# Tokens in the order of their groups: two tiles normed among the experts, two at the end

## The chip, the cores and the metric

The kernel runs on one core of a Trainium2 chip. The metric is the device time of one launch in microseconds (us). The core has a matrix engine, TensorE (PE, with its weight loads PEld), and VectorE (DVE), ScalarE (ACT) and GpSimd (POOL); SyncE (SP) issues most transfers, and 16 DMA engines move them. Each engine and each queue works its instructions off in order; engines wait for one another by semaphores. SBUF is the memory beside the engines (128 partitions), PSUM takes TensorE's results (banks of 512 fp32 columns on 128 partitions).

## The reference

One layer of an encoder over 512 tokens of 1024 values in fp32, normed after each part: two kinds of attention and their projections, a norm, and then a mixture of experts and the second norm. What matters here is the second half:

```python
def _hierarchical_moe(x, ...):          # x: 512 x 1024, after the first norm
    g_sel = top_k(softmax(x @ w_group + b_group), 1)          # 1 group of 4, its probability g_val
    top_w = softmax(top_k(e_logits of that group, 2))         # 2 experts of its 8
    for g in range(4):
        hid = silu(x @ w_gate[g]) * (x @ w_up[g])             # 8 experts, 256 wide
        y = y + (hid * combine[:, g]) @ w_down[g]
x = _layer_norm(ALPHA * x + y, ln2_g, ln2_b)
```

A token thus goes to two experts of one group. The 32 experts' weights (3 MB each, 96 MB in all) are all read.

## The kernel before

The attention part, the first norm and the routing take the first 410 us or so and stay as they are, apart from a few rows of the routing. The normed tokens (over ALPHA's scale, with what the end needs) lie in `hD` in DRAM, by token. `finish_routing()` works out for each expert the list of its tokens (at most 64 slots; more in any expert sets `flag`, and a dense way is then taken at the end). `toki` and `rowi` hold, for each pair of experts `p` (128 slots), the row in `hD` that a slot reads and the row in `y2D` that it writes. `y2D` has two rows for each token, one for each of its experts, zeroed at the start.

The experts follow in order, `for e in range(NE)`. Their weights come as six loads of 512 KB each: four for gate and up, two for down, in the order of the list `seq`, issued by SP and with `AHEAD` loads allowed ahead (`weights`, `raw_load`). For an expert TensorE does `gate_up(e)` (16 matmuls into a bank `sc`; ACT and DVE bring it out and add its halves into `gus`), `down(e - 1)` (8 matmuls into `tr`; ACT and DVE bring it out, scaled by the routing weight, into `oe`), at every odd expert `prep_x` (the gathered rows `xg` of the next pair are transposed into a bank `pj`, and ACT and DVE copy it to `xp`), and `act(e)` (four transposes of `gus` into `stp`, then `sg`, SiLU on ACT and a product on DVE). GpSimd gathers `xg` for a later pair (`fetch`) and after each pair scatters `oe` to `y2D`. `pin` and `in_order` fix the order of instructions; what isn't pinned the scheduler may place. The last two pairs (experts 28 to 31) don't go through DRAM: their results `late` stay in SBUF, and matmuls by one-hot matrices `stl` add them to their tokens.

The end works by tiles of 128 tokens. SP loads the residual rows `hb` of the four tiles after expert 20's part of the program (`HB_AT`) and, behind all weights, the eight tiles of rows `yy` of `y2D` (`last_rows`). Eight PSUM banks `fin` hold the four tiles (two banks a tile). An order written out by hand, `FIN`, adds into them by matmuls: `hb` by the identity, `late` of each of the four last experts by `stl`, and the sum of a tile's two `yy` tiles, added on GpSimd for tiles 0 to 2 and left to the matmuls for tile 3. Behind each tile comes its norm: statistics, root and two gain steps on DVE (`stat`, `gain`, `root`), the root's Ln and Exp on ACT; the last step of tiles 0 to 2 is on ACT and GpSimd, of tile 3 on DVE. SP writes the tiles out.

Of the kernel before, what the change touches and what calls it, by code (L numbers as in the profile page):

```python
# [94 lines left out]
).split()  # L95
# [10 lines left out]
def trunk(ctx, tc, xT, x, wm, wv, wbr, wout, wr, br, bg, rbx, lnp, lncol, wexp, out):  # L106
# [36 lines left out]
    hD = dram.tile([S, D], F32, name="hD")  # L143

# [522 lines left out]
    val = small([P, TT, 2], "val", at=end0)  # L667
    tokv = small([P, TT, 2], "tokv", at=end0)
# [59 lines left out]
    iota([P, TT, 2], [[2 * P, TT], [1, 2]], -2 * S, 2, "val", val)  # L728
# [145 lines left out]
    def route(tt):  # L874
# [7 lines left out]
        m = small([P, 4], f"m{tt}")  # L882
# [20 lines left out]
        mm(rk, tri, MS[:, tt, :], False, True)  # L903
        pm = small([P, 2, NE], f"pm{tt}")
# [12 lines left out]
    def finish_routing():  # L917
# [10 lines left out]

        pmf = B8[:, :2].rearrange("p q t k n -> p (q t k n)").rearrange("p (k t e) -> p k t e", k=2, t=TT)
# [33 lines left out]
        cn = pp.tile([P, NE], F32, tag="av", name="cn", bufs=AVB)  # L963
        for u in range(TT):
            mm(cn, ones, MS[:, u, :], u == 0, u == TT - 1)
        V.tensor_reduce(out=mx, in_=cn, axis=AX.X, op=OP.max)
        V.tensor_scalar(out=flag, in0=mx, scalar1=CAP + 0.5, scalar2=None, op0=OP.is_gt)
# [72 lines left out]
    for e in range(NE + 1):  # L1040
        seq += [(e, c) for c in range(4) if e < NE] + [(e - 1, 4 + f) for f in range(2) if e > 0]
# [79 lines left out]
    def gate_up(e):  # L1121
# [11 lines left out]
        nc.scalar.activation(gus[e], ps[CAP:], AF.Copy)  # L1133
        nc.vector.tensor_add(gus[e], gus[e], ps[:CAP])  # L1134
# [3 lines left out]
    def act(e):  # L1138
# [13 lines left out]
    def down(e):  # L1152
# [21 lines left out]
        if odd and p < NPAIR - NLATE:  # L1174
            nc.gpsimd.indirect_dma_start(  # L1175
                out=y2D[:, :], out_offset=bass.IndirectOffsetOnAxis(ap=rowi[:, p : p + 1], axis=0),
                in_=oe[p], in_offset=None, bounds_check=2 * S - 1, oob_is_err=False,
            )

    res, fs, fr, fu, parts = {}, {}, {}, {}, {}  # L1180
    stl = []
    gb2 = []
    late = []

    def last_rows():

        tok3 = bp.tile([P, 2 * NLATE], F32, tag="tok3", name="tok3", bufs=1)
        nc.vector.tensor_scalar(out=tok3, in0=tok2, scalar1=-256.0, scalar2=None, op0=OP.add)
        for n in range(NLATE):
            st = lop.tile([P, 2, 2, 256], F32R, tag="lo", name=f"stl{n}")  # L1190
            for k in range(2):
                i = k * NLATE + n
                for q, tok in enumerate((tok2, tok3)):
                    nc.vector.tensor_scalar(
                        out=st[:, k, q], in0=iota256, scalar1=tok[:, i : i + 1], scalar2=None, op0=OP.is_equal
                    )
                stl.append(st[:, k].rearrange("p q s -> p (q s)"))
        for tt in range(TT):
            y2.append([slot([P, D], F32, f"yy{tt}{k}") for k in range(2)])
            for k in range(2):  # L1200
                nc.sync.dma_start(y2[tt][k], y2v[tt, k])
# [14 lines left out]
    y2, hb = [], []  # L1216
    fin, added = {}, {}

    def fin_open(n):
        tt, cs = n // 2, slice(n % 2 * S, n % 2 * S + S)  # L1220
        fin[n] = pb.tile([P, S], F32, tag=FIN_TAG[n], name=f"fin{n}", bufs=NBUF[FIN_TAG[n]])
        mm(fin[n], ident, hb[tt][:, cs], True, False)
        added[n] = 0
# [225 lines left out]
```

## Time and profile before

| | |
|---|---|
| median of the runs | 688.9 us (688.48 to 690.85, 3 runs) |
| the profiled execution | 689.27 us, its span 687.6 us |
| busy in the span | PE 647.6 us (94%), DVE 393.4 (57%), ACT 312.1 (45%), POOL 102.5 (15%) |
| mean granted clock of TensorE | 0.985 |
| DMA | 160.17 MB, mean 233 GB/s; SP's queue 152.26 MB, POOL's 7.31 MB |

The span runs from the first to the last instruction; the run's time has some more around it. Busy shares are means over stages that differ: the DMA moves little in the first half and 400 GB/s and more among the experts.

### The profile page before, as it was taken

What the parts mean: (1) busy time and instruction counts of PE and PEld (TensorE: products, weight loads), DVE (VectorE), ACT (ScalarE), POOL (GpSimd) and SP (SyncE); (2) the same over time, 40 slices, a digit from 0 to 9 for tenths busy, and PEclk for the clock granted to TensorE, in tenths of its full rate; (3) what the DMA queues carried; (4) which work ended last, traced back from release to release, by engine and by line L of the source; (5) the groups of instructions that cost most, each with busy time, mean ns of one, the idle gap of its engine ahead of it and who ended that gap; (6) DMA issues with size and microseconds to landing.
All of it is one profiled execution on the core that took longest, in us unless ns stands there. A gap on an engine that the chain in (4) does not pass through costs nothing.

```text
span 687.6 us, 8900 instructions
## 1 busy us (share of the span) xinstructions
PE 647.6 (94%) x3128; PEld 422.8 (61%) x3128; DVE 393.4 (57%) x820; ACT 312.1 (45%) x618; POOL 102.5 (15%) x149
## 2 busy tenths in 40 slices
PE   8999999999999999989999988999999988899992
PEld 4888788887878888878888775343333422223351
DVE  5675868678867887563854994233233322224256
ACT  5676877866755665644523222222222322222232
POOL 2012112102010110050000331211111111000043
PEclk9999999999999999999999999899999999999997
DMA  8600069103130322126793579999999999999923
GB/s 329 253 1 0 1 227 353 63 0 93 47 107 17 123 76 93 37 97 260 264 362 125 177 290 399 407 410 409 409 411 407 408 408 408 402 411 409 407 96 123
DMA packets 48320, 160.17 MB, mean 233 GB/s; under 512 B 7438, under 2 KB 7582, under 8 KB 48272
## 3 DMA queue, kind: packets, MB, share of 16 engines
q1 hardware_dynamic: 44208, 152.26, 58.0%
q0 software_dynamic: 4064, 7.31, 2.8%
q8 instruction: 26, 0.43, 0.3%
q14 instruction: 22, 0.18, 0.1%
HBM read 151.20 MB, written 15.73 MB: 243 GB/s over the span
## 4 chain that ended last, share of the span: by engine, by line
PE 60%; DVE 15%; DMA 14%; ACT 6%; issue 3%; POOL 0%; SPq 0%; DVEq 0%; POOLq 0%; ACTq 0%
PE pj L132 18%; PE sc L132 13%; DMA we<-in_wexp_dram 11%; PE pb L132 6%; PE tr L132 6%; PE po L132 4%; PE pv L132 2%; PE fin L132 2%; PE av L132 2%; DVE t L484 2%; DVE wl L117 2%; DMA hb<-hD 2%; PE tr L538 2%; DMA raw<-in_wm_dram 2%; ACT wh L114 1%
## 5 line engine op out<-in xcount | busy, mean ns | idle before, releaser
L132 PE MATMUL sc<-we,xp 128*64 128x512 f32 x448 | 107.8, 604 | 4.0 <-DMA we<-in_wexp_dram 3.4
L132 PE MATMUL pj<-xh,wh 128*128 128x512 f32 x256 | 103.5, 404 | 1.2 <-ACT wh L114 1.1
L132 PE MATMUL pj<-xh,wl 128*128 128x512 f32 x256 | 101.0, 394 | 0.2 <-DVE wl L117 0.2
L132 PE MATMUL pj<-xl,wh 128*128 128x512 f32 x256 | 100.9, 394 | 0.2 <-DVE xl L117 0.2
L117 DVE TENSOR_TENSOR wl<-raw,wh 128x1024 fp32r<-128x1024 f32 (+1 forms) x57 | 69.9, 1231 | 22.8 <-ACT wh L114 22.6
L1134 DVE TENSOR_TENSOR gus<-gus,sc 64x512 f32<-64x512 f32 x32 | 21.7, 679 | 97.7 <-ACT gus L1133 97.7
L132 PE MATMUL tr<-we,sg 128*64 128x512 f32 x256 | 64.5, 614 | 6.9 <-DMA we<-in_wexp_dram 5.1
L1133 ACT ACTIVATE gus<-sc 64x512 f32<-64x512 f32 x32 | 19.0, 593 | 109.2 <-PE sc L132 109.2
L114 ACT ACTIVATE wh<-raw 128x1024 fp32r<-128x1024 f32 (+1 forms) x57 | 58.7, 1037 | 18.8 <-DMA raw<-in_wbr_dram 4.8
L132 PEld LDWEIGHTS sc<-we,xp 128*64 128x64 f32 x448 | 27.5, 136 | 59.5 <-issue 29.0
L132 PEld LDWEIGHTS pj<-xh,wl 128*128 128x128 f32 x256 | 48.4, 189 | 11.5 <-DVE wl L117 1.1
L132 PEld LDWEIGHTS pj<-xh,wh 128*128 128x128 f32 x256 | 48.5, 189 | 10.8 <-ACT wh L114 1.6
L132 PEld LDWEIGHTS pj<-xl,wh 128*128 128x128 f32 x256 | 48.5, 190 | 9.1 <-DVE xl L117 0.9
L132 PEld LDWEIGHTS tr<-we,sg 128*64 128x64 f32 x256 | 16.9, 139 | 47.1 <-issue 32.3
L132 PE MATMUL pb<-y,wh 128*128 128x512 f32 x128 | 40.0, 394 | 0.3 <-DVE k L347 0.3
L117 DVE TENSOR_TENSOR wl<-tr,wh 128x512 fp32r<-128x512 f32 (+1 forms) x64 | 30.9, 485 | 11.9 <-ACT wh L114 11.6
L491 POOL TENSOR_SCALAR_AFFINE_SELECT w<-w 128x128 f32<-128x128 f32 x32 | 16.1, 514 | 125.5 <-ACT w L488 117.8
L114 ACT ACTIVATE wh<-tr 128x512 fp32r<-128x512 f32 (+1 forms) x64 | 27.2, 427 | 12.4 <-PE tr L538 12.2
L1175 POOL DMA_INDIRECT y2D<-oe,rowi x14 | 14.1, 1010 | 118.9 <-DVE oe L1173 91.4
L132 PE MATMUL sc<-k,q 128*128 128x512 f32 (+3 forms) x128 | 28.5, 323 | 0.2
L538 PE MATMUL tr<-ident,w 128*128 128x128 f32 x160 | 27.8, 272 | 0.0
L132 PEld LDWEIGHTS pb<-y,wh 128*128 128x128 f32 x128 | 23.3, 188 | 5.0 <-PE tr L538 0.5
(226 smaller groups left out, 1188.1 us busy)
## 6 DMA issues: line engine op xcount, KB each, us to landing
we<-in_wexp_dram SPq DMA_DIRECT2D x192, 512.0 KB, 11.2
raw<-in_wm_dram SPq DMA_DIRECT2D x32, 512.0 KB, 6.2
raw<-in_wv_dram SPq DMA_DIRECT2D x8, 512.0 KB, 8.7
y2D<-zero SPq DMA_DIRECT2D x16, 256.0 KB, 4.2
raw<-in_wbr_dram SPq DMA_DIRECT2D x8, 512.0 KB, 5.0
raw<-in_wout_dram SPq DMA_DIRECT2D x8, 512.0 KB, 4.9
yy<-y2D SPq DMA_DIRECT2D x8, 512.0 KB, 10.1
strip<-in_rbx_dram SPq DMA_DIRECT2D x8, 256.0 KB, 4.7
```

The lines of the kernel that those rows point to most:

```text
L114: act = nc.scalar.activation(hi, src, AF.Copy)
L117: pin((eng or nc.vector).tensor_sub(lo, src, hi.bitcast(F32)), fix == "both")
L132: pin(nc.tensor.matmul(ps, a, b, start=start, stop=stop))
L484: nc.vector.tensor_tensor_scan(out=t[:, ::-1], data0=t[:, ::-1], data1=mk[:, ::-1], initial=0.0, op0=OP.add, op1=OP.mult)
L491: nc.gpsimd.affine_select(out=blk, in_=blk, pattern=[[-1, P]], compare_op=OP.is_gt, fill=0.0, base=0, channel_multiplier=1)
L538: nc.tensor.transpose(tr[:, i * P : (i + 1) * P], w[:, off + j * P : off + (j + 1) * P], ident)
L1133: nc.scalar.activation(gus[e], ps[CAP:], AF.Copy)
L1134: nc.vector.tensor_add(gus[e], gus[e], ps[:CAP])
L1175: nc.gpsimd.indirect_dma_start(out=y2D[:, :], out_offset=bass.IndirectOffsetOnAxis(ap=rowi[:, p : p + 1], axis=0), in_=oe[p], in_offset=No ...
```

## The change

Positions of tokens are now sorted by group: the routing counts the tokens of each group, and a token's position is the number of tokens in earlier groups plus its rank among its own. `y2D`'s rows, the one-hot matrices for the late experts and the tiles of the end go by positions. So tiles 0 and 1 hold tokens of the first groups only, whose experts are done long before the end. `tokD` in DRAM keeps which token stands at a position (four small scatters at experts 4 to 10, read back at 13 as `tokp`). All row loads move from SP to GpSimd's queue: residual rows are gathered by `tokp`, tiles 0 and 1 with their `y2D` rows at experts 23 and 26, tiles 2 and 3 at 28 and 29. Tiles 0 and 1 are summed and normed on DVE at experts 26 and 28 and scattered to the output by GpSimd; only tiles 2 and 3 stay for the end, with four banks, into which the late experts and, for each tile, one sum of rows are added. The last three experts' down weights are loaded behind expert 31's gate and up weights. Outputs of `gate_up`, `act` are now pinned. The dense way is also taken where the first two groups have under 128 tokens or the first three under 256.

```diff
+ROWS_AT = {23: 0, 26: 1}
+NORM_AT = {26: 0, 28: 1}
+GAIN_AT = 21
+OUT_AT = {28: 0, 30: 1}
+TOKD_AT = {4: 0, 6: 1, 8: 2, 10: 3}
+TOKP_AT = 13
...
+        cn = pp.tile([P, NE], F32, tag="av", name="cn", bufs=AVB)
+        for u in range(TT):
+            mm(cn, ones, MS[:, u, :], u == 0, u == TT - 1)
+        V.tensor_reduce(out=cg, in_=cn.rearrange("p (g e) -> p g e", g=4), axis=AX.X, op=OP.add)
...
+        V.tensor_add(p2[:, 0], p2[:, 0], p2[:, 1])
+        V.tensor_tensor(out=val, in0=last(p2[:, 0], 2), in1=k01, op=OP.add)
...
-    for e in range(NE + 1):
-        seq += [(e, c) for c in range(4) if e < NE] + [(e - 1, 4 + f) for f in range(2) if e > 0]
+    for e in range(NE):
+        seq += [(e, c) for c in range(4)] + [(e - 1, 4 + f) for f in range(2) if 0 < e < NE - 2]
+    seq += [(e, 4 + f) for e in range(NE - 3, NE) for f in range(2)]
...
-        nc.scalar.activation(gus[e], ps[CAP:], AF.Copy)
-        nc.vector.tensor_add(gus[e], gus[e], ps[:CAP])
+        pin(nc.scalar.activation(gus[e], ps[CAP:], AF.Copy))
+        pin(nc.vector.tensor_add(gus[e], gus[e], ps[:CAP]))
...
-                nc.sync.dma_start(y2[tt][k], y2v[tt, k])
...
+    def tile_rows(tt, pool):
+        for y, k, where in ((ya, 0, pool), (yb, 1, slots2)):
+            y[tt] = slot([P, D], F32, f"y{k}{tt}", where)
+            tc.keep_in_program_order(nc.gpsimd.dma_start(y[tt], y2v[tt, k]))
...
+    def tile_sum(tt, eng):
+        pin(eng.tensor_add(ya[tt], ya[tt], hb[tt]))
+        pin(eng.tensor_add(ya[tt], ya[tt], yb[tt]))
...
+        act(e)
+        if e in ROWS_AT:
+            tile_res(ROWS_AT[e])
+            tile_rows(ROWS_AT[e], slots2)
+        if e in NORM_AT:
+            t = NORM_AT[e]
+            tile_sum(t, nc.vector)
+            tile_norm(t, (ya[t][:, :S], ya[t][:, S:]), "vector")
+        if e in OUT_AT:
+            tile_out(OUT_AT[e])
...
+    tile_sum(2, nc.vector)
+    tile_sum(3, nc.gpsimd)
+    down(NE - 2)
...
+    for n in range(2):
+        mm(fin[n], ident, ya[2][:, n * S : n * S + S], False, False)
+    down(NE - 1)
```

On DVE, the first place is experts 26 and 27. Before, the sum `gus` of expert 26 is the first row and that of expert 27 the fourth; the copy `xp` for experts 28 and 29 comes behind both:

```order
L1134 TENSOR_TENSOR gus<-gus,sc 64x512
L1173 TENSOR_SCALAR oe<-tr,wslot 64x512
L1147 TENSOR_TENSOR sg<-sg,stp 128x128
L1134 TENSOR_TENSOR gus<-gus,sc 64x512
L1173 TENSOR_SCALAR oe<-tr,wswap 64x512
L1088 COPY xp_5457<-pj 128x512
L1147 TENSOR_TENSOR sg<-sg,stp 128x128
```

After, `gus`, `oe` and `sg` of expert 26 are as before (not shown), and then comes this, where `y_5434` is tile 0 (the rows of its first expert, to which its residual `hb_5430` and the rows of its second expert `y_5436` are added):

```order
L1122 COPY xp_5592<-pj 128x512
L1258 TENSOR_TENSOR y_5434<-y_5434,hb_5430 128x1024
L1259 TENSOR_TENSOR y_5434<-y_5434,y_5436 128x1024
L1268 BN_STATS bsf<-y_5434 128x6 x2
L1269 BN_AGGR mv<-bsf 128x2
L1270 TENSOR_SCALAR mv<-mv 128x1
L1274 SCALAR_TENSOR_TENSOR y_5434<-y_5434,mv,gb_5274 128x512 x2
L1277 SCALAR_TENSOR_TENSOR mv<-mv 128x1
L1278 TENSOR_SCALAR mv<-mv 128x1
L1279 TENSOR_TENSOR mv<-mv 128x1
L1285 SCALAR_TENSOR_TENSOR y_5434<-y_5434,mv,gb_5303 128x512 x2
L1168 TENSOR_TENSOR gus<-gus,sc 64x512
```

The copy `xp` has moved from behind expert 27's `gus` to ahead of tile 0's eleven rows, and `gus` of expert 27, the last row here, stands behind them all.

On GpSimd, the end of the expert loop before: the last gather, three scatters of pairs, and the sums of `yy` of three tiles:

```order
L1092 DMA xg_3019<-hD,toki 128x1024
L1175 DMA y2D<-oe,rowi 1024x1024 x3
L1242 TENSOR_TENSOR yy_5578<-yy_5578,yy_5579 128x1024
L1242 TENSOR_TENSOR yy_5582<-yy_5582,yy_5583 128x1024
L1242 TENSOR_TENSOR yy_5586<-yy_5586,yy_5587 128x1024
```

After, from the last gather (`hb_5430`, `y_5434`, `y_5436` belong to tile 0, `hb_5547`, `y_5551`, `y_5553` to tile 1, the next two to tiles 2 and 3):

```order
L1126 DMA xg_3027<-hD,toki 128x1024
L1251 DMA hb_5430<-hD,tokp 128x1024
L1247 DMA y_5434<-y2D 128x1024
L1247 DMA y_5436<-y2D 128x1024
L1251 DMA hb_5547<-hD,tokp 128x1024
L1208 DMA y2D<-oe,rowi 1024x1024 x2
L1290 DMA out_dram<-y_5434,tokp 512x1024
L1247 DMA y_5551<-y2D 128x1024
L1247 DMA y_5553<-y2D 128x1024
L1251 DMA hb_5672<-hD,tokp 128x1024
L1251 DMA hb_5676<-hD,tokp 128x1024
L1208 DMA y2D<-oe,rowi 1024x1024
```

Row loads that stood in SP's queue now stand between gathers and scatters. Tile 0's output (`out_dram`) is ahead of tile 1's rows, and the scatter of a pair is behind both.

On PE, the end after, from the transposes of the last expert's `gus` (`we_5439` is the down weight of expert 30, `we_5447` that of 31, `y_5723` tile 2):

```order
L1175 MATMUL stp<-ident,gus 128x64 x4
L125 MATMUL tr<-we_5439,sg 64x512 x2
L125 MATMUL tr<-we_5443,sg 64x512 x2
L125 MATMUL fin_5743<-late_5774,stl 128x512
L125 MATMUL fin_5745<-late_5774,stl 128x512
L125 MATMUL fin_5747<-late_5774,stl 128x512
L125 MATMUL fin_5749<-late_5774,stl 128x512
L125 MATMUL fin_5743<-y_5723,ident 128x512
L125 MATMUL fin_5745<-y_5723,ident 128x512
L125 MATMUL tr<-we_5447,sg 64x512 x2
```

Tile 2's two identity matmuls stand ahead of the down matmuls of expert 31; before, in that place, stood nothing between the down matmuls of experts 30 and 31.

## Rows read from the trace of the kernel before

**Rows 1.** Windows of the experts' stretch and of one us after the last load.
```profile
420.00:640.00 220.00, 206.18 (x998) 73.90 (x996) 67.81 (x134) 57.90 (x116) 28.36 (x28) 0.98 1.03 408
...
662.00:663.00 1.00, 1.00 (x5) 0.63 (x4) 0.00 (x0) 0.00 (x0) 0.08 (x1) 1.00 0.00 0
```

**Rows 2.** PE's timeline, experts 4 to 6: start, us, engine, line, operation, tiles.
```profile
447.94 1.09 PE L1107 MATMUL pj<-ident,xg 128*128 128x128 f32 x8
...
455.04 3.65 PE L132 MATMUL sc<-we,xp 128*64 128x512 f32 x16
458.52 1.89 PE L132 MATMUL tr<-we,sg 128*64 128x512 f32 x8
460.34 1.09 PE L1107 MATMUL pj<-ident,xg 128*128 128x128 f32 x8
```

**Rows 3.** SP's timeline from 400 us: its DMA issues.
```profile
410.03 197.01 SPq L1052 DMA_DIRECT2D we<-in_wexp_dram  x142
607.97 4.08 SPq L1327 DMA_DIRECT2D hb<-hD  x4
614.19 27.90 SPq L1052 DMA_DIRECT2D we<-in_wexp_dram  x22
643.04 9.29 SPq L1201 DMA_DIRECT2D yy<-y2D  x8
```

**Rows 4.** DMA issues: size of one, median us from issue to landing.
```profile
we<-in_wexp_dram SPq DMA_DIRECT2D x192, 512.0 KB, 11.2
...
yy<-y2D SPq DMA_DIRECT2D x8, 512.0 KB, 10.1
...
out_dram<-res SPq DMA_DIRECT2D x3, 512.0 KB, 2.6
...
xg<-hD,toki POOLq DMA_INDIRECT x14, 7.3
```

**Rows 5.** DVE's timeline of the end.
```profile
659.55 0.76 DVE L120 SCALAR_TENSOR_TENSOR late<-tr,wslot,late 64x512 fp32r<-64x512 f32 x1 [0.75 <-ACT late L119]
664.45 0.70 DVE L1264 BATCH_NORM_STATS2 bsf<-fin 128x6 f32<-128x512 f32 x1 [4.14 <-PE fin L132]
...
667.05 0.21 DVE L787 SCALAR_TENSOR_TENSOR mv<-mv 128x1 f32<-128x1 f32 x1
...
668.10 0.69 DVE L1264 BATCH_NORM_STATS2 bsf<-fin 128x6 f32<-128x512 f32 x1
...
678.93 1.12 DVE L787 SCALAR_TENSOR_TENSOR mv<-mv 128x1 f32<-128x1 f32 x1
...
681.01 1.41 DVE L1290 SCALAR_TENSOR_TENSOR res<-res,mv,gb 128x512 f32<-128x512 f32 x2
```

**Rows 6.** POOL's timeline: the first gather, the last one, adds at the end.
```profile
430.66 1.10 POOL L1092 DMA_INDIRECT xg<-hD,toki  x1 [14.51 <-DVE rowi L949]
...
580.78 1.01 POOL L1092 DMA_INDIRECT xg<-hD,toki  x1 [6.35 <-PE pj L1107]
...
677.55 2.48 POOL L1299 TENSOR_TENSOR res<-res,gb 128x512 f32<-128x512 f32 x2 [1.76 <-ACT res L1298]
```

**Rows 7.** PE's timeline, experts 26 and 27, and expert 31's down.
```profile
610.61 2.22 PE L132 MATMUL tr<-we,sg 128*64 128x512 f32 x8 [0.29 <-DMA we<-in_wexp_dram]
...
613.79 0.46 PE L1141 MATMUL stp<-ident,gus 64*128 64x64 f32 x4
...
655.35 1.94 PE L132 MATMUL tr<-we,sg 128*64 128x512 f32 x8 [1.49 <-DVE sg L1147]
```

**Rows 8.** Groups of instructions by form, DVE: adds of 128x1024 from SBUF.
```profile
L117 DVE TENSOR_TENSOR wl<-raw,wh 128x1024 fp32r<-128x1024 f32 x55 | 68.7, 1251 | 22.3 <-ACT wh L114 22.1
```

**Rows 9.** ACT's timeline of the end: a table load.
```profile
654.38 1.28 ACT L1145 ACT_TABLE_LOAD   x1
```

**Rows 10.** Windows with the granted clock, after two idle times of PE.
```profile
431.00:437.00 6.00, 5.19 (x18) 1.75 (x20) 1.49 (x6) 1.74 (x7) 2.74 (x3) 0.50 1.03 408
...
654.00:656.00 2.00, 0.65 (x4) 0.34 (x6) 1.03 (x2) 1.97 (x4) 1.31 (x1) 1.00 0.99 393
```

More of the change, by code (lines that the diff above doesn't have):

```diff
@@ L962, in finish_routing @@
         nc.scalar.activation(wswap[HD:, :], wslot[:HD, :], AF.Copy)
[L963 to L967, printed above, removed]
+        V.tensor_scalar(out=posf, in0=p2[:, 0], scalar1=0.5, scalar2=1.0 * S, op0=OP.mult, op1=OP.add)
+        V.tensor_scalar(out=mx, in0=mx, scalar1=CAP + 0.5, scalar2=None, op0=OP.is_gt)
+        for k, n in ((2, 2 * P), (3, 4 * P)):
+            V.tensor_scalar(out=few[:, k - 2 : k - 1], in0=sp[:, k : k + 1], scalar1=n - 0.5, scalar2=None, op0=OP.is_lt)
+            V.tensor_tensor(out=mx, in0=mx, in1=few[:, k - 2 : k - 1], op=OP.max)
+        V.tensor_scalar(out=flag, in0=mx, scalar1=0.5, scalar2=None, op0=OP.is_gt)
         for tt in range(TT):
@@ L1174, in down @@
         if odd and p < NPAIR - NLATE:
-            nc.gpsimd.indirect_dma_start(
+            tc.keep_in_program_order(nc.gpsimd.indirect_dma_start(
                 out=y2D[:, :], out_offset=bass.IndirectOffsetOnAxis(ap=rowi[:, p : p + 1], axis=0),
                 in_=oe[p], in_offset=None, bounds_check=2 * S - 1, oob_is_err=False,
[L1178 to L1200, printed above, removed]
-                nc.sync.dma_start(y2[tt][k], y2v[tt, k])
+            ))
+    late, gb2, stl = [], [], []
     def gain_rows():
@@ L1214, in gain_rows @@
                 nc.scalar.activation(gb2[k][:, j * S : j * S + S], ps, AF.Copy)
[L1216 to L1223, printed above, removed]
-    def fin_add(n, upto):
-        tt, cs = n // 2, slice(n % 2 * S, n % 2 * S + S)
-        for k in range(added[n], upto):
-            end = k == 2 * NLATE - 1 and FIN.index(f"add{n}.{k + 1}") > FIN.index(f"rows{tt}")
-            mm(fin[n], stl[k][:, tt * P : (tt + 1) * P], late[k][:, cs], False, end)
-        added[n] = upto
@@ new lines, in late_slots @@
+    def late_slots():
+        st = lop.tile([P, 2 * NLATE, 2 * P], F32R, tag="lo", name="stl")
+        for n in range(NLATE):
+            for k in range(2):
+                i = k * NLATE + n
+                one = st[:, 2 * n + k]
+                V.tensor_scalar(out=one, in0=iota256, scalar1=tok2[:, i : i + 1], scalar2=None, op0=OP.is_equal)
+                V.scalar_tensor_tensor(
+                    out=one, in0=iota256, scalar=tok3[:, i : i + 1], in1=one.bitcast(F32), op0=OP.is_equal, op1=OP.add
+                )
+                stl.append(st[:, 2 * n + k])
@@ new lines, in tile_out, with fin_add @@
+    def tile_out(tt):
+        tc.keep_in_program_order(nc.gpsimd.indirect_dma_start(
+            out=out[:, :], out_offset=bass.IndirectOffsetOnAxis(ap=tokp[:, tt : tt + 1], axis=0),
+            in_=ya[tt], in_offset=None, bounds_check=S - 1, oob_is_err=False,
+        ))
+    fin = []
+    def fin_add(n, k):
+        if len(fin) <= n:
+            fin.append(pb.tile([P, S], F32, tag=FIN_TAG[n], name=f"fin{n}", bufs=NBUF[FIN_TAG[n]]))
+        mm(fin[n], stl[k][:, n // 2 * P : (n // 2 + 1) * P], late[k][:, n % 2 * S : n % 2 * S + S], k == 0, k == 2 * NLATE - 1)
```

203 lines of the change are left out of this document (109 added, 94 removed), and 6 rows, old and new, of the table FIN.

## The prediction

> **What bounds the kernel now.** I read the windows first, because the experts are a stage of their own. From 420 to 640 us the DMA engines are busy all the time at 408 GB/s [rows 1], and TensorE (PE) idles only in short waits for a weight tile. A 512 KB load therefore takes 524,288 / 408,000 = 1.285 us of the core's DMA time, and a pair of experts (12 loads) 15.4 us, while PE, where the weights are there, does a pair in 12.4 us (from one transpose of gathered rows to the next, 447.94 to 460.34) [rows 2]. So PE has a slack of some 3 us a pair, or a little more once PE's own waits are counted, and whatever is loaded extra ahead of a weight pushes PE back by 1.285 us.
>
> SP's timeline says what stands in that stream: the weights to 642.09, with four residual loads (hb) at 607.97 among them, and behind them eight row loads (yy) from 643.04 [rows 3]. These are issued to 652.3 and land after 10.1 us [rows 4]; in 662 to 663 us nothing moves any more [rows 1]. The weights are thus in long before the rows, and what ends last is PE's adding into the eight banks and then VectorE (DVE): first statistics at 664.45, the next tile's at 668.10 (3.65 us a tile, without a wait), the last end from 681.01 to 682.42 [rows 5]. That is 18.0 us of DVE behind the first statistics, for four tiles. The span ends 5.2 us after DVE's last row (687.6), the output's way out; the run is 1.67 us longer than the span.
>
> **Part 1: the row loads move ahead of the weights.** The last xg gather issues at 580.78 [rows 6], and in the new order the loads hb, y, y, hb of tiles 0 and 1 stand right behind it. They wait for nothing that comes later than the scatter before it, so they issue at about 582 to 586 and cost 4 × 1.285 = 5.1 us ahead of the weights of experts 26 and 27 (before, hb came only behind those of 27). With about 1.0 us for the small token transfers at experts 4 to 13 and for the front (bounds: nothing, and 2.6, two loads' time), tr(26), which runs from 610.61 to 612.8 [rows 7], ends at 618.9. The transposes behind it end at 619.9, and the copy xp for experts 28 and 29 on DVE at 620.7 (bank to SBUF, about as long as a statistic's 0.7).
>
> The routing chain grows by some fifteen small DVE rows; at 0.21 a row, what the root's small row took alone [rows 5], and with what waits between engines, that is about 4 us, so the first gather moves from 430.66 [rows 6] to 434.8. Its rows are wanted at 447.94 [rows 2], and a gather lands after 7.3 us [rows 4], so 5.8 us of cover stay. PE's resumption in that stretch does move, but the loads issued ahead keep the DMA busy, so I cost it at nothing; with that cover gone it is up to 4.1 us.
>
> **Part 2: norm 0 stands in DVE's way.** The new order puts the norm of tile 0 behind the copy xp, which waits for PE's transposes, and ahead of gus(27). PE, after those transposes, wants stp(27), which reads gus(27). Before, stp(27) ran at 613.79 without a wait [rows 7]. The norm: two 128x1024 adds at 1.25 [rows 8] = 2.5; statistics to root 3.65 [rows 5]; a table load of 1.28 on ScalarE between Ln and Exp [rows 9], of which the two gain rows hide about half, 0.65; the end 1.41 [rows 5]. Sum 8.2 us (7.6 if the table load is hidden whole, 8.8 if not at all). DVE is through at 628.9, gus(27) at 629.6, stp(27) starts at 629.7: PE stands still for 9.8 us.
>
> Then the clock. After PE had little to do around 430 us, the granted clock was 0.50 for six us (1.2 GHz of 2.4), although PE worked; an idle time of 1.49 us at 653.9 left it at 1.00 [rows 7, 10]. So after 9.8 us I expect the low level for a part of what follows, and take sc(28) at 5.5 us, midway between 3.65 [rows 2] and its double 7.3 (all of it low: +1.8). stp(27) .9, sc(28) to 636.1, tr(27) 1.9, stp(28) to 638.5, sg(28) on DVE to 639.3.
>
> **Part 3: tile 1.** GpSimd's queue holds the scatter of tile 0's output ahead of tile 1's two row loads, and that scatter waits for norm 0 (628.9). At 1.0 us an issue [rows 6] they go out to 632 and land 6.8 to 8.8 us after their issue (as gathers do; median 7.3 [rows 4]), 638.8 to 640.8. Norm 1 starts at about 639.6, ends at 647.8 and gus(29) at 648.5. PE meanwhile has sc(29), tr(28), transposes, to 645.2, and waits 3.3 us: stp(29) .9, sc(30) 4.6 (between 3.65 and 5.5, since this idle time lies between those two), to 654.0. Then four late adds 1.2, stp(30) .5, sc(31) 3.6, tr(29) 1.9, stp(31) .5: 661.7.
>
> **Part 4: the tail.** Behind sg(31) and the split of expert 29 (3.0 us behind its matmuls, as before from 657.29 to 660.31 [rows 5, 7]) DVE is free at 664.4, and adds tile 2's rows: 666.9. PE's two ident matmuls for them stand ahead of tr(31) in its order: 667.9, then tr(31) to 669.8, the split to 672.8, the last adds to the first bank 0.6: 673.4. That is 9.0 us later than the 664.45 of before, though the 16 yy/hb adds on PE are gone. From there two tiles: 3.5 + (3.5 + 1.4) = 8.4, and 0.3 for what tile 3's root loses beside GpSimd's adds for tile 2: its row took 0.21 alone and 1.12 while GpSimd was adding [rows 5, 6]. DVE ends at 682.1 (before 682.42).
>
> What the rows show there is also a rule of the Trainium skill ("SBUF — State Buffer", section "SBUF: two separate sides"): VectorE and GpSimd share a port pair, and an operation with two SBUF inputs is shut out for the whole length of the other's. By that rule alone the sums of tiles 2 (VectorE) and 3 (GpSimd), if they meet, would run one after the other, at most two GpSimd adds longer; I expect them apart, as tile 3's rows are in by about 655.
>
> The output goes from GpSimd by rows instead of from SP: issue 1.0 instead of 0.5 us, and 1.2 us more for landing, since gathers and scatters took longer than the direct store's 2.6 [rows 4] (bounds: no more than before, 0, and 7.3 − 2.6 = 4.7 in all). I take +1.7. Span 682.1 + 5.2 + 1.7 = **689.0**; with 1.67 the run is 690.7 against the profiled 689.27. That execution is 0.37 above the median of 688.9, so the number on the runs' scale is **690.3 us**. So the tail gets 9.3 us shorter and begins 9.0 later: of 6.1 (weights later), 9.8 and 3.3 (PE held) and about 3 (clock), 13 are made up by PE's slack and by adds that it no longer does.
>
> **The rivals.**
>
> *The DMA sets the end (faster).* PE may make up all but the weights' delay, if norm 0 is shorter or the clock comes back at once. Then the last weight counts: 662.2 before as the last transfer, + 2.6 for two tiles written earlier (1 MB) + 0.7 for tokens = 665.5. Behind it .95 (half of tr(31)), 3.0, .6, 8.7, and 6.9 for the way out: span 685.6, on the scale 686.9; with the output as cheap as before 685.2. It decides when PE's chain is 2.4 us shorter (tr(31) starting at 665.5 instead of 667.9). For it: the two lie close. Against it: both norms stand in DVE's order ahead of a gus that PE needs.
>
> *The low clock lasts (slower).* Six us at 0.50 [rows 10] cost 3 us for work at full load. I counted 1.9 + .4 for sc(28) and stp(27), 1.4 for the second. If both holds bring the full stretch at 0.50, that adds 2 × 1.6 = 3.2: span 692.2, **693.5**. It decides when the windows after stp(27) and stp(29) show 0.50 for over 5 us each. Against it: the clock may already be low while PE stands still.
>
> *The front pays (slower).* If the later routing leaves the DMA without work, all is up to 4.1 us later: 694.4. SP has ten us of loads outstanding there, so this is small.
>
> *The change does not do what it says.* Tile 0 needs 128 tokens in the first two groups, and tile 1 256 in the first three, or a dense way is taken; the inputs put 123, 132, 127 and 130 tokens into the groups, so it isn't. No chance worth a number.
>
> **How the numbers follow.** The forecast's own range is 688.5 to 691.5, by the landing of the output (−1.7 to +1.3 of it) and norm 0's 0.6 either way. Chances: forecast .45, DMA sets the end .25, low clock lasts .25, front .05. A measurement of this kernel tells 0.3% (2.1 us): within it are 686.8 to 691.0. Of the forecast .33 lies within and .12 above (its end at 691.5); of the DMA case .2 lies below 686.8, since the output's cost is more likely counted too high than too low there, and .05 within; forecast cases with a cheap output add .03 below, taken from within; of the low clock .05 lies within. Together faster .23, same .40, slower .37. The range 685.2 to 694.0 takes in the DMA case and nearly all of the low clock.
>
> **What the changed profile would show.** Part 1: tr(26)'s start about 6 us later. Part 2: PE idle for 8 to 11 us before stp of expert 27, released by DVE's gus, with ACT table loads around the norms; if PE does not wait there, this part is wrong and the time falls towards 685. Part 3: tile 1's row loads issued behind the scatter of tile 0. Part 4: first bank statistics near 673, DVE's end near 682, the span's end 6 to 7 us behind it. The prediction is wrong above all if PE makes up more than its three pairs give, or if DVE waits for rows that land late.

## The result and the profile after

The changed kernel takes **706.85 us** (median of 4 runs, 705.63 to 710.17) against 688.69 (685.55 to 690.85) for the kernel before on the same chip: a ratio of 1.0275 [1.0221, 1.0329]. The forecast was 690.3, within 685.2 to 694.0. It is wrong by 16.6 us, and slower than every rival allowed.

The profiled execution took 710.17 us, 3.3 above the median, its span 708.5, at a mean granted clock of 0.961. I read it against the prediction's own landmarks. First the windows among the experts, with the columns of [rows 1]: length, busy time of PE, PEld, DVE, ACT and POOL, then the granted clock, the DMA share and GB/s.

```profile
440.00:460.00 20.00, 20.00 (x104) 7.41 (x102) 6.00 (x11) 5.84 (x12) 4.05 (x4) 1.00 1.03 407
460.00:508.00 48.00, 48.00 (x252) 18.53 (x250) 16.39 (x28) 14.04 (x30) 11.50 (x12) 1.00 1.02 316
460.00:464.00 4.00, 4.00 (x26) 1.83 (x24) 2.27 (x4) 1.44 (x3) 1.04 (x1) 1.00 1.15 221
...
496.00:500.00 4.00, 4.00 (x26) 1.86 (x24) 1.71 (x3) 2.04 (x4) 0.58 (x1) 1.00 1.29 297
500.00:504.00 4.00, 4.00 (x22) 1.39 (x20) 0.90 (x3) 0.59 (x1) 0.46 (x1) 1.00 0.77 236
508.00:600.00 92.00, 83.04 (x398) 28.87 (x396) 28.82 (x62) 22.97 (x44) 14.48 (x16) 1.00 1.03 407
```

From 460 to 508 us the DMA engines are as busy as ever (share 1.02) and move only 316 GB/s; ahead of it and behind it they move 407. In the short windows the rate falls to 221 to 310. Each dip covers two of them: in the first the share is over 1 (1.13 to 1.29), in the second under it (0.77 to 0.90). At 408 GB/s, the rate of [rows 1], those 48 us are worth (408 − 316) × 48 / 408 = 10.8 us of the weights' stream. PE shows nothing of it there (48.00 of 48 busy), since it still has weights ahead. POOL's timeline of the stretch says what is new in it:

```profile
454.51 1.01 POOL L1316 DMA_INDIRECT tokD<-toks,posi  x1 [3.69 <-ACT posi L1314]
...
466.91 1.01 POOL L1316 DMA_INDIRECT tokD<-toks,posi  x1 [3.67 <-ACT posi L1314]
...
479.32 1.01 POOL L1316 DMA_INDIRECT tokD<-toks,posi  x1 [3.68 <-DMA y2D<-oe,rowi]
...
491.73 1.01 POOL L1316 DMA_INDIRECT tokD<-toks,posi  x1 [3.35 <-ACT posi L1314]
```

Four scatters of 128 tokens of 4 bytes each, 512 bytes in one scatter; each dip begins four to six us behind the start of one of them, and the scatter lands after 8.6 us (median of the four). Then PE's timeline: its first transposes of gathered rows, as in [rows 2], and from expert 26's down matmuls on:

```profile
448.42 1.09 PE L1141 MATMUL pj<-ident,xg 128*128 128x128 f32 x8
...
627.73 2.24 PE L125 MATMUL tr<-we,sg 128*64 128x512 f32 x8 [0.29 <-DMA we<-in_wexp_dram]
629.91 1.09 PE L1141 MATMUL pj<-ident,xg 128*128 128x128 f32 x8
640.25 0.69 PE L1175 MATMUL stp<-ident,gus 64*128 64x64 f32 x4 [9.25 <-DVE gus L1168]
640.87 6.12 PE L125 MATMUL sc<-we,xp 128*64 128x512 f32 x16
...
660.72 0.69 PE L1175 MATMUL stp<-ident,gus 64*128 64x64 f32 x4 [5.30 <-DVE gus L1168]
661.34 6.13 PE L125 MATMUL sc<-we,xp 128*64 128x512 f32 x16
...
681.09 3.78 PE L125 MATMUL fin<-y,ident 128*128 128x512 f32 x4 [2.43 <-DVE y L1259]
684.80 2.93 PE L125 MATMUL tr<-we,sg 128*64 128x512 f32 x8
```

tr(26) starts at 627.73, 17.1 us later than the 610.61 of [rows 7], where 6.1 were forecast. The two holds are there: 9.25 us before stp(27), 5.30 before stp(29), both released by DVE's gus. DVE's rows around them and at the end:

```profile
631.04 0.69 DVE L1122 COPY xp<-pj 128x512 f32<-128x512 f32 x1 [6.04 <-PE pj L1141]
...
639.53 0.67 DVE L1168 TENSOR_TENSOR gus<-gus,sc 64x512 f32<-64x512 f32 x1
...
652.88 1.23 DVE L1259 TENSOR_TENSOR y<-y,y 128x1024 f32<-128x1024 f32 x1 [1.19 <-DMA y<-y2D]
...
677.88 1.89 DVE L1258 TENSOR_TENSOR y<-y,hb 128x1024 f32<-128x1024 f32 x1
...
690.84 1.29 DVE L1268 BATCH_NORM_STATS2 bsf<-fin 128x6 f32<-128x512 f32 x2
...
698.15 1.42 DVE L1285 SCALAR_TENSOR_TENSOR y<-y,mv,gb 128x512 f32<-128x512 f32 x2
```

The first statistics of the end stand at 690.84 (before 664.45 [rows 5]), the last DVE row ends at 699.57, and the span ends 8.9 us later. POOL's rows say why so late, and the windows what the clock did:

```profile
639.89 0.98 POOL L1290 DMA_INDIRECT out_dram<-y,tokp  x1 [13.93 <-DVE y L1285]
640.85 1.17 POOL L1247 DMA_DIRECT2D y<-y2D  x2
...
698.31 1.49 POOL L1290 DMA_INDIRECT out_dram<-y,tokp  x1 [0.60 <-POOL y L1283]
703.25 0.98 POOL L1290 DMA_INDIRECT out_dram<-y,tokp  x1 [3.45 <-DMA out_dram<-y,tokp]
```

```profile
630.00:640.00 10.00, 1.00 (x8) 0.76 (x8) 8.36 (x15) 6.07 (x8) 0.11 (x1) 0.78 1.02 399
640.00:650.00 10.00, 9.75 (x38) 3.40 (x40) 2.44 (x5) 2.22 (x6) 4.10 (x5) 0.71 1.01 403
...
680.00:690.00 10.00, 8.91 (x20) 3.39 (x21) 3.29 (x5) 2.05 (x3) 0.00 (x0) 0.66 0.00 1
```

Tile 3's output is issued at 703.25, 3.45 us after POOL was free and 3.7 after DVE's last row; by the profile it waits for tile 2's output to land in the same tensor.

Laid beside the forecast's span of 689.0, the 19.5 us divide by landmarks: 11.0 up to tr(26); −0.5 to stp(27) (12.5 us after tr(26), forecast 13.0); +3.0 from there to sg(31); +0.6 for tile 2's sum; +3.3 from the sum to the first statistics; nothing for the two tiles (8.73, forecast 8.7); +2.0 for the way out.

### The profile page after: what moved, and what is told of

It is laid out like the page before. It is cut to its first block, busy times and chain, and to the rows that moved or that the text cites. A ratio compares the mean times of both kernels' runs of the same rounds, so it can differ in the third digit from the quotient of the medians.

```text
span 708.5 us, 8862 instructions
## 1 busy us (share of the span) xinstructions
PE 641.7 (91%) x3084; PEld 417.6 (59%) x3084; DVE 404.6 (57%) x850; ACT 319.2 (45%) x628; POOL 115.1 (16%) x167
## 4 chain that ended last, share of the span: by engine, by line
PE 51%; DMA 20%; DVE 17%; ACT 7%; issue 3%; POOL 1%; SPq 0%; POOLq 0%; DVEq 0%; ACTq 0%
DMA we<-in_wexp_dram 16%; PE pj L125 15%; PE sc L125 11%; PE pb L125 6%; PE tr L125 4%; PE po L125 4%; DVE t L478 3%; DVE wl L110 2%; PE pv L125 2%; PE av L125 2%; ACT wh L107 2%; DMA y<-y2D 2%; DMA raw<-in_wm_dram 2%; DVE t L476 1%; PE tr L532 1%
## 5 line engine op out<-in xcount | busy, mean ns | idle before, releaser
L125 PE MATMUL sc<-we,xp 128*64 128x512 f32 x448 | 112.6, 631 | 5.8 <-DMA we<-in_wexp_dram 4.7
L125 PE MATMUL tr<-we,sg 128*64 128x512 f32 x256 | 66.0, 625 | 8.1 <-DMA we<-in_wexp_dram 7.7
L125 PEld LDWEIGHTS sc<-we,xp 128*64 128x64 f32 x448 | 29.1, 142 | 66.8 <-DMA we<-in_wexp_dram 31.9
L1175 PEld LDWEIGHTS stp<-ident,gus 64*128 64x128 f32 x128 | 11.1, 147 | 34.0 <-DVE gus L1168 27.8
L1175 PE MATMUL stp<-ident,gus 64*128 64x64 f32 x128 | 15.6, 246 | 16.3 <-DVE gus L1168 16.3
```

Of the source, the lines that this page charges most:

```text
L125: pin(nc.tensor.matmul(ps, a, b, start=start, stop=stop))
L1175: pin(nc.tensor.transpose(st[:, q, :], gus[e][:, q * P : (q + 1) * P], ident[:CAP, :CAP]))
```

## The experiments

The main theory was that the token scatters take the 11 us, the rival that the norms in DVE's order do. Times are medians; the kernel before ran in each set beside them (688.58, 688.39, 689.01 and 689.02 us in the four sets). The differences from the changed kernel are against its 706.85. The sets ran on different chips, and the kernel before ties them together.

**1. Without the token scatters.** `tokp` is written by an iota instead.

```diff
+    nc.gpsimd.iota(tokp, pattern=[[P, TT]], base=0, channel_multiplier=1)
...
-        if e in TOKD_AT:
+        if e in ():
```

> The changed kernel without the four token scatters into tokD and without its load: tokp is filled with 0 to 511 instead, so the output rows stand in the wrong places; all other work is the same. Theory A (each scatter of 128 pieces of 4 bytes takes about 2.8 us of the weights' DMA time, 11 us for four): the windows from 460 to 504 us show 408 GB/s throughout, the down matmuls of expert 26 start near 616.7 instead of 627.7, and the time falls from 706.9 to about 696 (694 to 698). Rival (the dips come from something else there, such as the scatters of the experts' rows): the dips stay, 705 to 708.

694.83 us (693.56 to 699.36), ratio to before 1.0109 [1.0068, 1.0151]: 12.0 less than the changed kernel, and 409 GB/s from 460 to 508 us. The scatters, with the reading back of `tokD`, are the larger part of the loss. (Without them the outputs go to the wrong rows; the work is the same.)

**2. Pieces of 512 bytes.** Each token is written 128 times over, a row of 512 bytes.

```diff
-    tokD = dram.tile([S, 1], I32, name="tokD")
+    tokD = dram.tile([S, P], I32, name="tokD")
...
-                in_=toks[:, t : t + 1], in_offset=None, bounds_check=S - 1, oob_is_err=False,
+                in_=toks, in_offset=None, bounds_check=S - 1, oob_is_err=False,
```

> The changed kernel with token rows of 512 bytes instead of 4 in tokD: the same four scatters of 128 pieces each, the number repeated 128 times. Theory A1 (it is the size of the piece that costs): the dips in the DMA rate go, although 128 times as many bytes are written (256 KB, about 0.6 us): about 696 to 697. Theory A2 (any scatter of 128 pieces at this place costs 2.8 us, whatever its size): the dips stay, 706 to 708.

700.04 us (696.14 to 703.46), 1.0177 [1.0124, 1.0229]. The dips are gone (409 GB/s), with as many pieces and 128 times the bytes, so neither the number of pieces nor their bytes makes them. How much that gives back this run doesn't settle, since its executions spread over 7 us, with mean clocks of 0.951 to 0.964.

**3. Without the sums and norms of tiles 0 and 1.** The scatters stay; the two tiles' rows go out unnormed.

```diff
-        if e in NORM_AT:
+        if e in ():
```

> The changed kernel without the sums and norms of tiles 0 and 1 (their rows go out unnormed); token scatters stay. Theory B (the two norms in VectorE's order hold TensorE for 9.3 + 5.3 us, and the low clock behind each costs 2 to 2.5 more): TensorE's waits for gus vanish and the end is set by the last weight, which landed at about 671.5: + 0.95 + 3.0 + 0.6 + 8.7 + 8.9 us behind it and 1.7 around the span gives 695.4 (693 to 698). Rival (TensorE makes up for the holds anyway, the end is late for another reason): 703 or more.

703.71 us (702.99 to 708.98), 1.0246 [1.0203, 1.0290]: only 3.1 less. Its waits of PE (us in total, times, longest):

```profile
PE sc L125 <- DMA we<-in_wexp_dram: 16.8, 22, 1.5
PE tr L125 <- DMA we<-in_wexp_dram: 8.1, 15, 1.6
...
PE stp L1175 <- DVE gus L1168: 1.7, 2, 1.4
```

In the changed kernel these are 4.7, 7.7 and 16.3. The 14.6 us of holds have gone, and 12.5 us of waits for weights stand in their place: while PE was held, the late weights were coming in. So the holds cost little as long as the DMA is behind, and the expectation, which took them as a cost of their own, was wrong.

**4. The norms in two pieces.** Sums on GpSimd, statistics and end of a norm at different experts, so that no gus waits for a whole norm.

```diff
-NORM_AT = {26: 0, 28: 1}
+SUM_AT = {25: 0, 27: 1}
+STATS_AT = {26: 0, 29: 1}
+END_AT = {27: 0, 30: 1}
...
-OUT_AT = {28: 0, 30: 1}
+OUT_AT = {29: 0, 31: 1}
```

> The changed kernel, complete, with all work of the norms of tiles 0 and 1 but in other places: the sums on GpSimd, the norm in two pieces behind sg of experts 26 and 27 (tile 0) and 29 and 30 (tile 1), the copies xp and oe kept in program order, one table load ahead of Ln, and the outputs behind the rows of the next tiles. Theory B: as without the norms, or up to 2 us more: 695 to 698. Rival (VectorE's time itself, 5.6 us a tile, is what is missing, wherever it stands): 702 or more.

703.22 us (702.09 to 710.34), 1.0240 [1.0179, 1.0302]: the same as leaving the norms out.

**5. The scatters alone, in the kernel before.** Four scatters of 4-byte pieces at experts 4, 6, 8 and 10, position p · 4 + t, so that the pieces of one scatter land 16 bytes apart. The times are those of the kernel before with this added:

```diff
+    tokD = dram.tile([S, 1], I32, name="tokD")
...
+    nc.gpsimd.iota(perm, pattern=[[1, TT]], base=0, channel_multiplier=TT)
...
+        if e in (4, 6, 8, 10):
...
+                out=tokD[:, :], out_offset=bass.IndirectOffsetOnAxis(ap=posi[:, t : t + 1], axis=0),
```

> The kernel before with nothing added but four scatters of 128 pieces of 4 bytes at experts 4, 6, 8 and 10 (a fixed permutation of 0 to 511, into a tensor that nobody reads) and the four small ScalarE copies ahead of them; the order on all engines is otherwise the same. Theory A (the scatter itself takes 2.8 us of the weights' DMA time): the dips in the DMA rate appear between 455 and 505 us, and the time rises from 688.6 by 10 to 12, to about 699. Rival (the dips need something else of the change): 688 to 690.

686.86 us (685.89 to 687.33), 0.9975 [0.9954, 0.9996]: no dip (408 GB/s) and no loss, against the expectation. So a scatter of 4-byte pieces is not dear as such here. What was left that differed was where the pieces land: in the changed kernel a tile's tokens of one group get neighbouring positions, so the pieces come in four runs that touch.

**6. Pieces of 64 bytes** in the changed kernel (`tokD` 16 wide).

```diff
+    tokD = dram.tile([S, 16], I32, name="tokD")
```

> The changed kernel with token rows of 64 bytes in tokD, otherwise as with 512 bytes. If every piece under 512 bytes costs about as much as one of 4 bytes, the dips stay: 705 to 708. If the cost goes with smaller pieces only, the dips go or shrink: 696 to 702.

696.78 us (695.75 to 698.20), 1.0103 [1.0054, 1.0153]: 10.1 less, no dips.

**7. The same scatters in the kernel before, close together.** One line differs from experiment 5: the pieces of one scatter are now 128 neighbours.

```diff
-    nc.gpsimd.iota(perm, pattern=[[1, TT]], base=0, channel_multiplier=TT)
+    nc.gpsimd.iota(perm, pattern=[[P, TT]], base=0, channel_multiplier=1)
```

> The kernel before plus the same four token scatters as in the run with them alone, but each piece of 4 bytes goes right behind its neighbour's (the place of a token is its own number) instead of 16 bytes from it. Theory A3 (4-byte pieces that fall close together hinder each other, and the weights with them): the dips in the DMA rate appear between 455 and 505 us, and the time rises by 8 to 12, to 696 to 700. Rival (closeness does nothing): 686 to 689, as with 16 bytes between them.

706.30 us (705.16 to 707.34), 1.0231 [1.0166, 1.0296]: 17.3 above the kernel before. Its windows, against one of experiment 5 (first fence):

```profile
460.00:508.00 48.00, 48.00 (x250) 18.56 (x248) 16.54 (x28) 14.59 (x31) 11.09 (x11) 1.00 1.03 408
```

```profile
460.00:508.00 48.00, 44.99 (x226) 16.25 (x224) 14.13 (x24) 13.16 (x28) 10.04 (x10) 1.00 0.99 274
...
472.00:476.00 4.00, 4.00 (x22) 1.38 (x20) 0.97 (x2) 1.64 (x4) 1.00 (x1) 1.00 0.64 141
...
496.00:500.00 4.00, 2.69 (x14) 0.83 (x12) 0.68 (x1) 0.59 (x1) 0.00 (x0) 1.00 0.76 148
```

And the landing of the scatters, spread and then close (issue, count, median us to landing):

```profile
tokD<-toks,posi POOLq DMA_INDIRECT x4, 5.9
```

```profile
tokD<-toks,posi POOLq DMA_INDIRECT x4, 11.7
```

Same bytes, same number of pieces, same issues: only the addresses differ, and with them some 19 us (706.30 against 686.86). More than expected, and 4.3 a scatter instead of the changed kernel's 2.7 (its 10.8 us by four), whose runs are shorter. No run has pieces between touching and 16 bytes apart, so whether they have to touch, or only to lie closer than that, is not shown.

**8. The changed kernel with its 4-byte pieces 64 bytes apart.**

```diff
-    tokD = dram.tile([S, 1], I32, name="tokD")
+    tokD = dram.tile([16 * S, 1], I32, name="tokD")
...
+            pin(nc.scalar.activation(posi[:, t : t + 1], posf[:, t : t + 1], AF.Copy, scale=16.0))
```

> The changed kernel with pieces of 4 bytes as they are, but 64 bytes apart in tokD (the position times 16). Theory A3 (closeness): the dips go, 695 to 700, as with wide rows. Rival A1 (the size of the piece of 4 bytes): the dips stay, 705 to 708.

696.86 us (694.99 to 702.54), 1.0107 [1.0070, 1.0144]: 10.0 less, the same as with 64-byte pieces and, within about 2 us, as with none at all. It is the changed kernel with nothing altered but the addresses of `tokD`, so its trace is the one to lay beside the forecast; its rows stand in the next section.

**9 to 11. What is left.** Three steps on wide pieces. First the norms in pieces as in experiment 4 (e5); then tile 2's sum moved to behind gus(31) (e6); then also all of tiles 2's and 3's adds on PE behind the last down matmuls, and tile 2's last step on DVE (e9).

```diff
+        if e == NE - 1:
+            tile_sum(2, nc.vector)
...
+    for k in (1, 2):
+        for n in range(4):
+            fin_add(n, k)
...
-    tile_norm(2, fin[:2], "both")
+    tile_norm(2, fin[:2], "vector")
```

> Both remedies at once, complete: token rows of 512 bytes, and the norms of tiles 0 and 1 in pieces with their sums on GpSimd. With the DMA free of the dips the weights are in at about 660, and with the same way behind it as in the run with pieces alone (13.6 us from the end of the transfers to the first statistics, then 8.7, 8.9 and 1.7) the time is about 692 (690 to 694). Rival (once the weights come earlier, TensorE's holds are hidden and their removal gives nothing): 696 to 700, as with wide rows alone.

> The run before this one, and VectorE's two adds for tile 2 moved from behind sg of expert 31 to behind gus of expert 31, so that TensorE's identity matmuls and the last down matmuls need not wait for them. Theory C (in the tail, the adds of tile 2 hold expert 31's down matmuls back, though their weights are there: 5 us in the run with pieces): 687 to 689. Rival (the last weights set the start of those matmuls anyway): 691 to 693, no change.

> The run with wide rows, pieces and the early sum, and the tail in another order: TensorE does all adds into the four banks behind expert 31's down matmuls, and tile 2's last step is on VectorE instead of ScalarE and GpSimd, so that its output leaves some 3 us earlier and tile 3's output, which waits for it to land, too. Theory D (what is left beside the kernel before, 693 against 688.4, is the order of the tail and the wait of one output for the other): 687 to 689. Rival (the low clock and the last weights set it): 691 to 694.

693.95 us (691.83 to 696.69), 1.0069 [1.0040, 1.0098]; 693.20 (690.61 to 698.34), 1.0072 [1.0038, 1.0106]; and 690.21 (688.15 to 696.42), 1.0000 [0.9966, 1.0033]. Without the dips too, taking the holds away gives only 2.8 us (e5 against experiment 6, whose pieces have 64 bytes; against experiment 2, with the same pieces as e5, it is 6.1, but that run's executions spread over 7 us). The earlier sum alone gives nothing that is clear of the spread; DVE's and POOL's timelines of e6 show what met:

```profile
657.26 2.77 DVE L1259 TENSOR_TENSOR y<-y,hb 128x1024 f32<-128x1024 f32 x1
660.07 3.25 DVE L1260 TENSOR_TENSOR y<-y,y 128x1024 f32<-128x1024 f32 x1
```

```profile
656.61 2.34 POOL L1259 TENSOR_TENSOR y<-y,hb 128x1024 f32<-128x1024 f32 x1 [3.05 <-DMA y<-y2D]
659.50 2.73 POOL L1260 TENSOR_TENSOR y<-y,y 128x1024 f32<-128x1024 f32 x1 [0.56 <-DMA y<-y2D]
```

An add that takes 1.22 us on DVE alone took 2.77 and 3.25 beside POOL's. Counted from the end of POOL's add, 658.95 + 1.22 = 660.17 and 662.23 + 1.22 = 663.45, it should end within 0.15 us of where it did (660.03, 663.32): DVE's add did its work behind POOL's, not beside it.

Of what e9 has over e6, 3.0 us by the medians, one wait can be read in the profiles. In e6 tile 3's output is issued 3.8 us behind DVE's last row, which ends at 682.86, and waits for tile 2's to land; in e9, where tile 2's goes out earlier, it is issued 0.8 behind DVE's last row (688.65) and waits for DVE alone (first fence e6, second e9). From DVE's end to the end of the span it is 8.8 us in e6 and 6.0 in e9. What the other order of the adds gave or took is not shown apart.

```profile
686.61 0.97 POOL L1304 DMA_INDIRECT out_dram<-y,tokp  x1 [4.13 <-DMA out_dram<-y,tokp]
```

```profile
689.44 0.97 POOL L1304 DMA_INDIRECT out_dram<-y,tokp  x1 [4.13 <-DVEq L1396]
```

**12 to 14. Where the tail's gain went.** All on e9. Outputs of tiles 0 and 1 issued behind the sum of the last rows, so that nothing competes with the last weights (e10); that with the weight order of before, and tile 2's sum again behind sg(31) (e11); and e10 with tile 3's output into another tensor, so that its rows are missing in the output (e12).

```diff
+    with tc.issue_after(tile_sum(3, nc.gpsimd)):
+        tile_out(0)
+        tile_out(1)
```

```diff
+            out=(outD if tt == 3 else out)[:, :], out_offset=bass.IndirectOffsetOnAxis(ap=tokp[:, tt : tt + 1], axis=0),
```

> The run before this one with the outputs of tiles 0 and 1 sent behind the last rows' sum on GpSimd, when the weights are in, instead of among them. By the DMA's rate they cost 2 x 1.29 us ahead of the last weights: 2 to 3 us less than the run before, 684.5 to 687. Rival (they fill gaps, or the chain of outputs then ends later): no change or slower.

> The run with late outputs, with the weights in the order of the kernel before (each expert's down weights behind the next expert's gate and up weights, so that only expert 31's come last) and tile 2's adds again behind sg of expert 31, ahead of which nothing waits for them now. Theory E (with three experts' down weights behind the last gate and up weights, TensorE has three downs, a transpose and the low clock left when the last weight lands; in the old order one down): first statistics 5 to 7 us earlier, 684 to 687. Rival (the last weight's landing alone counts, whichever it is): 690 to 691.

> The run with late outputs, with tile 3's output scattered into another DRAM tensor, so that it has no earlier write to wait for (its rows are then missing in the output). Theory F (tile 3's output waits 3.5 to 4 us for tile 2's to land, and the span with it): 3 to 4 us less, 686.5 to 688. Rival (the way out takes as long anyway): 690 to 691.

690.88 us (688.51 to 692.73), 1.0006 [0.9976, 1.0037]: no difference from e9. 691.32 (689.36 to 697.77), 1.0027 [0.9992, 1.0062]: none either. The first statistics stand at 673.87 instead of e10's 674.65, where 5 to 7 us less were expected, so the theory that the down weights at the end cost the time falls. PE's row there shows the new wait in its place: ahead of expert 31's down matmuls it is idle for 3.00 us behind DVE, and then at the low clock (granted 0.52 from 664.5 to 668; 3.57 us for a row that takes 1.89 to 1.94 elsewhere):

```profile
664.56 3.57 PE L127 MATMUL tr<-we,sg 128*64 128x512 f32 x8 [3.00 <-DVE sg L1180]
```

With the tensor apart 688.86 us (687.38 to 697.87), 0.9997 [0.9966, 1.0028]: by the medians 2.0 less than e10, where 3 to 4 were expected, and the two intervals overlap. The traces show no gain at that place. In e10 too the last issue waits for DVE and not for the landing: it stands 0.8 us behind the end of DVE's last row, as in e12 (first fence e10, second e12):

```profile
683.20 1.41 DVE L1297 SCALAR_TENSOR_TENSOR y<-y,mv,gb 128x512 f32<-128x512 f32 x2
...
685.40 0.97 POOL L1306 DMA_INDIRECT out_dram<-y,tokp  x1 [4.18 <-DVEq L1400]
```

```profile
680.66 1.42 DVE L1298 SCALAR_TENSOR_TENSOR y<-y,mv,gb 128x512 f32<-128x512 f32 x2
...
682.86 0.96 POOL L1307 DMA_INDIRECT outD<-y,tokp  x1 [4.19 <-DVEq L1401]
```

From DVE's end to the end of the span it is 6.0 us in e10 and 6.2 in e12. What e12 is ahead in its profile lies before the first statistics (672.12 against 674.65), and already its first gather goes out 2.2 us earlier (433.76 against 435.94). So theory F fails here: the wait was gone since e9.

**15. The weight order of before alone,** on experiment 8.

```diff
-    for e in range(NE):
-        seq += [(e, c) for c in range(4)] + [(e - 1, 4 + f) for f in range(2) if 0 < e < NE - 2]
-    seq += [(e, 4 + f) for e in range(NE - 3, NE) for f in range(2)]
+    for e in range(NE + 1):
+        seq += [(e, c) for c in range(4) if e < NE] + [(e - 1, 4 + f) for f in range(2) if e > 0]
```

> The changed kernel with token pieces 64 bytes apart (696.9), with nothing else changed but the weights' order, which is that of the kernel before. Theory E: 691 to 695. Rival (with the norms holding TensorE, the weights' order makes no difference): 696 to 698.

696.79 us (695.52 to 697.48), 1.0108 [1.0045, 1.0171]: no difference from 696.86.

## Why the prediction was wrong

**The step that failed** is in Part 1: "about 1.0 us for the small token transfers ... and for the front (bounds: nothing, and 2.6, two loads' time)". The term was mis-sized by more than ten times. Counted from PE's first transposes of gathered rows (447.94 before [rows 2], 448.42 after), tr(26) comes 16.6 us later than before; in experiment 1, without the scatters, it comes 5.2 later (transposes at 446.80, tr(26) at 614.71). So the term measured 11.4 us there, and the run's time fell by 10.0 to 12.0 without it. Its upper bound failed too, since I priced the scatters by their bytes and number, as small work beside the loads of 512 KB. What costs is that the pieces of a scatter touch one another in DRAM (or lie closer than 16 bytes), and then it is the other transfers that pay. This is shown from both sides: apart in the changed kernel, −10.0; close in the kernel before, +17.3, and apart there, nothing. Nothing in the trace of before has such a scatter (its scatters write whole rows of 4 KB), so no row could have given the size; but the diff says that positions are sorted, and a bound from "no row like it" should have been wide.

How touching pieces slow the stream is not shown. The Trainium skill ("DMA: Bandwidth & Descriptors", section "Specifications") states that below 512 bytes a transfer is done as a read-modify-write. As stated there, the rule makes no difference between pieces that touch, pieces of 4 bytes that lie 16 or 64 bytes apart, and pieces of 64 bytes; here only the first make dips, and beside the others the DMA moves 408 to 409 GB/s from 460 to 508 us. So the rule does not explain the loss by itself. That touching pieces have to wait for one another's read and write would fit both, but no run shows it.

**The other steps held, up to the tail.** The tail is the second failure: experiment 8, which has the change without the dips, takes 696.86 us, so the forecast of 690.3 would have missed its range (up to 694.0) without the scatters too. PE's rows there read:

```profile
615.39 2.23 PE L125 MATMUL tr<-we,sg 128*64 128x512 f32 x8 [0.27 <-DMA we<-in_wexp_dram]
...
627.91 0.69 PE L1175 MATMUL stp<-ident,gus 64*128 64x64 f32 x4 [9.26 <-DVE gus L1168]
...
647.93 0.69 PE L1175 MATMUL stp<-ident,gus 64*128 64x64 f32 x4 [4.59 <-DVE gus L1168]
...
667.54 3.17 PE L125 MATMUL fin<-y,ident 128*128 128x512 f32 x4 [2.87 <-DVE y L1259]
670.64 2.40 PE L125 MATMUL tr<-we,sg 128*64 128x512 f32 x8
...
674.01 1.88 PE L125 MATMUL fin<-y,ident 128*128 128x512 f32 x4
```

- *Row loads ahead of the weights:* tr(26) is 4.8 us later than before, and 6.1 counted from the transposes (446.58 in this execution, which is 1.4 ahead from there on). The four loads were priced at 5.1 and measured 5.2 in experiment 1; spread out, the token transfers were then worth the 0.9 that is left, against the 1.0 of the forecast. The front is hidden, as forecast: the first gather goes out at 434.18 in the changed kernel (forecast 434.8), and PE's transposes behind it at 448.42 (before 447.94 [rows 2]).
- *Norm 0:* in the changed kernel 7.9 us of DVE (631.64 to 639.53, forecast 8.2), PE held 9.25 (9.8), and stp(27) in experiment 8 at 627.91 (629.7).
- *Tile 1:* its rows went out behind tile 0's output, and DVE's second add waited for them, 1.19 us in the changed kernel and 0.48 here; stp(29) at 647.93 (forecast 648.5), though the hold was 4.6 instead of 3.3. sg(31) is through at 664.0 (664.4).
- *The tail's length:* 8.73 us for two tiles, forecast 8.7.

What experiment 8's profiled span, 693.8, has beyond 689.0 lies in Part 4 all but −0.4 (about +1.0 if its start, 1.4 ahead, is taken out):

- *Tile 2's sum* on DVE took 3.6 us instead of 2.5, as it met GpSimd's adds, which I had expected apart (+1.1).
- *From the sum to the first statistics* it took 8.7 instead of 6.5 (+2.2). The ident row took 3.17 us where I had counted 1.0, and tr(31) 2.40 where I had counted 1.9. Part of this was a wrong price: the same row of tile 3 takes 1.88 at the full clock. The rest, 1.3 and 0.5, is the clock, which I had put at nothing in the tail: PE had stood idle for 2.87 us, and the granted clock was 0.68 from 667.5 to 669.5 and 0.50 from 669.5 to 671.5. Some 0.5 came back in the last adds.
- *The way out* took 8.9 instead of 6.9, with the second output waiting for the first to land (+2.0), a wait that the forecast did not have.

**The rivals.** *The low clock lasts* came true in the changed kernel, by its own sign: the granted clock was 0.50 to 0.53 from 640 to 646 us and 0.50 to 0.59 from 660.7 to 666.7. Behind both holds sc took 6.1 us (forecast 5.5 and 4.6), 2.1 more of its 3.2. *The front pays* is excluded by the landmark above. *The DMA sets the end* came true otherwise than meant: with the holds gone, PE waits for weights instead (12.5 us more in experiment 3), which is why the holds were worth about 3 us and not 13.

**Where the tail's gain went.** Two tiles less at the end are 9.3 us of DVE, and no version got them: the best are equal to the kernel before (e9 1.0000 [0.9966, 1.0033], e10 1.0006 [0.9976, 1.0037]). In e10 the first statistics stand at 674.65 against 664.45 [rows 5], so the tail begins 10.2 later (7.7 in e12's execution). Of that, the row loads ahead of the weights are measured (5.2 at tr(26), in experiment 1); they used to come behind all weights, where PE needed nothing more from the DMA. For the rest, the tail of e10 and e11 shows short waits for DVE and for weights with the low clock behind them, but no run took them away one by one, so how it divides stays open.

## What to carry to other kernels

Price a scatter of small pieces by where the pieces land: here pieces that touched slowed the other transfers in flight, by far more than their own bytes, and spacing them out cost next to nothing. When transfers set the pace, work taken out of another engine's wait comes back as a wait for the transfers; ask first whether the loads move ahead of what the path waits for, as moved row loads did here. And where two scatters at the end write one tensor, look whether the second waits for the first to land: it did in the changed kernel (3.45 us), and sending the first out earlier took the wait away in e9.

## What the runs showed of the hardware that was not expected

- Four scatters of 128 pieces of 4 bytes cost the run 17.3 us where the pieces are neighbours (4.3 each), 10 to 12 where they come in four runs (2.5 to 3 each). With pieces 16 or 64 bytes apart, or of 64 bytes, there is no dip, and at 16 bytes apart in the kernel before no loss either. In the four-us windows of the dips the DMA engines show busy shares from 0.77 to 1.29 (changed kernel) at rates down to 221 GB/s there and 141 in experiment 7.
- DVE's add of two SBUF tiles ended 1.1 us behind the end of GpSimd's add in both meetings of e6, and took 2.77 and 3.25 us instead of 1.22. That is the rule that the prediction quotes from the Trainium skill ("SBUF — State Buffer", section "SBUF: two separate sides"), and the trace agrees.
